# A two-layer decoder trunk on one core: seven products in every step of the middle MLP passes, with part of the weights' low parts made by adding DMAs

## The chip, the cores and the metric

The kernel runs on one core of a Trainium2 chip. The metric is the device time of one execution in microseconds, as the median of several runs. The profiled execution has a span, from its first to its last instruction, which is a few microseconds shorter than the time of a run.

The engines are called by the profile's short names: PE is the matrix engine TensorE and PEld its weight loads, DVE is VectorE, ACT is ScalarE, POOL is GpSimd and SP is SyncE, which issues most of the DMAs. PSUM is the memory that PE writes to, eight banks of 512 columns of float32; SBUF is the working memory; both have 128 partitions.

## What is computed

The input is 256 positions of width 2048, in float32. There are two layers: a gated short convolution and an MLP, then latent attention and an MLP. After each of the four sub-layers stands x <- LN(alpha * x + f(x)). What matters here is the MLP, of which there are two:

```
def sq_relu_mlp(x, w1, w2):
    return jnp.square(jax.nn.relu(x @ w1)) @ w2        # w1: 2048 x 8192, w2: 8192 x 2048

h = layer_norm(ALPHA * h + mix, ln_g[layer, 0], ln_b[layer, 0])
h = layer_norm(ALPHA * h + sq_relu_mlp(h, mlp_w1[layer], mlp_w2[layer]), ln_g[layer, 1], ln_b[layer, 1])
```

## The kernel before

**Precision by parts.** PE multiplies in the type float32r, which holds fewer bits than float32. Each operand is therefore split into a high part (the value rounded to float32r) and a low part (the value minus the high part), and a product is three matmuls: high by high, high by low, low by high. `split` (L125) makes the two parts: ACT casts the high part (L127), DVE subtracts (L128). For the weights this is done on the chip, for every half of 128 x 1024 numbers that is loaded.

**The stream of weights.** `stream` is the list of all weight pieces in the order of their use. `take` (L183) hands out the next one and, before that, emits the loading and splitting of the pieces that are up to LOOK = 5 steps ahead. A raw half lands in a ring of RAW = 5 buffers (`raws`), its two parts in a ring of WA = 8 pairs (`whl`). The loads are issued on SP's queue (L138), which is in order: a load waits there until its buffer is free.

**An MLP.** `mlp` (L575) runs over NQ = 8 slices q of the hidden dimension, 1024 columns each. A pass has two halves. In the first, `products` multiplies the input by w1 in eight chunks of 128 hidden columns; `hidden` (L713) reads each chunk from PSUM (`whole`, L355 and L356), applies relu and square (L718, L719) and splits the result. In the second half the hidden values are multiplied by the slice of w2 and added to the sums of the output, 256 x 2048.

**Passes with seven products.** In the passes q = 1 to 6 (FAST) a 2 x 2 block product uses seven block products instead of eight, in the manner of Strassen and Winograd. `form` (L703) builds the four sums and differences of the hidden values (S1 to S4). `prepare` (L141) builds those of the weights: a step of seven loads two raw halves, the blocks 11 and 22 in the one, 21 and 12 in the other; DVE forms T1 and T3 (L162), T2 (L166) and T4 (L169), and three pairs of 1024 columns and one of 512 are split. `fast_products` (L343) issues the seven products, each by `dot` (L297), three matmuls of 512 columns (L300, L302, L303). They go into seven sums named "1" to "7", one PSUM bank each. Four of these (OWN: "1", "5", "7", "6") are kept apart over the passes in a buffer `sums`, the others are kept in blocks of the accumulator `acc`; `fold` (L669) adds the four to the accumulator in the last pass.

**The two groups.** The 2048 output columns are worked on as two groups g of 1024. In every middle pass group 1 comes first, with four steps in the order MIXED = "sssp": three steps of seven ("s") and one plain step ("p") that multiplies the same operands with eight products, without the sums and differences; one of its matmuls is split in two. Then come four steps of seven for group 0. The partial sums change place at each switch: `resumed` (L608) copies a sum from SBUF into its PSUM bank (L612), `put_back` (L615) copies it back (L616), both on ACT, and `keep` (L618) adds it to SBUF on DVE (L624).

**The residual.** `xres` holds the residual stream, 128 x 16 x 256 float32, in SBUF throughout. In the first MLP `begin` (`prepare_chunks`, L798) scales and centres its chunks for the next layer norm during the last pass, and `to_wide` (L776) adds the MLP's output to them. In the second MLP `turn_residual` (L1024) brings it to the accumulator: PE transposes it (L1027) into PSUM, DVE adds it to `acc` (L1028). That is spread over the passes 1 to 4, eight transposes in each, after the first chunk.

**Order.** The order of the instructions on each engine is set by a scheduler that places them by their dependences; an engine then works through its own queue in order and waits where an operand or a buffer is not there yet.

## Time and profile before

| | |
|---|---|
| Runs (three) | 1997.85, 1999.94, 2000.18 us; median 1999.94 us |
| Span of the profiled execution | 1994.9 us |
| Mean granted clock of PE | 1.000 |
| Loads of raw halves of w2 for the steps of seven | 168 of 512 KB, median 3.9 us from issue to landing |
| Loads of the other MLP weights | 344 of 512 KB, median 4.5 us |
| Bytes moved by DMA | 385.85 MB |

A page of the profile gives the busy time of each engine, the chain of work that ended last, the groups of instructions and the DMA issues. Matmuls are pipelined, so the busy time of a single one (0.39 us for 512 columns) is longer than the distance from its start to the next one's start; distances are what counts. The same holds on a smaller scale for DVE and ACT. In the rows, a name such as `lo<-raw,hi` is the written tile and the tiles read, and L128 is line 128 of the kernel.

### The profile page before, as it was taken

What the parts mean: (1) busy time and instruction counts of PE and PEld (TensorE: products, weight loads), DVE (VectorE), ACT (ScalarE), POOL (GpSimd) and SP (SyncE); (2) the same over time, 40 slices, a digit from 0 to 9 for tenths busy, and PEclk for the clock granted to TensorE, in tenths of its full rate; (3) what the DMA queues carried; (4) which work ended last, traced back from release to release, by engine and by line L of the source; (5) the groups of instructions that cost most, each with busy time, mean ns of one, the idle gap of its engine ahead of it and who ended that gap; (6) DMA issues with size and microseconds to landing.
All of it is one profiled execution on the core that took longest, in us unless ns stands there. A gap on an engine that the chain in (4) does not pass through costs nothing.

```text
span 1994.9 us, 30180 instructions
## 1 busy us (share of the span) xinstructions
PE 1987.7 (100%) x11110; PEld 1737.2 (87%) x11110; DVE 1709.4 (86%) x2555; ACT 1354.9 (68%) x2154; POOL 2.3 (0%) x21
## 2 busy tenths in 40 slices
PE   9999999999999999999999999999999999999998
PEld 8888888988888888888889998898888888888886
DVE  8667667797999989989978988777899999999985
ACT  6444445586778778777756755558677787887772
POOL 0000000000000000000000000000000000000000
PEclk9999999999999999999999999999999999999999
DMA  8666666565657466574855543656464656656483
GB/s 318 205 191 187 190 190 190 179 193 157 212 170 251 148 216 221 177 243 147 281 171 159 170 140 123 201 180 195 146 233 155 232 161 220 222 178 233 150 269 130
DMA packets 106853, 385.85 MB, mean 193 GB/s; under 512 B 11857, under 2 KB 12625, under 8 KB 106449
## 3 DMA queue, kind: packets, MB, share of 16 engines
q1 hardware_dynamic: 106560, 383.79, 59.5%
q8 instruction: 87, 1.43, 0.3%
q14 instruction: 62, 0.50, 0.1%
q10 hardware_dynamic: 144, 0.13, 0.0%
HBM read 381.78 MB, written 2.10 MB: 192 GB/s over the span
## 4 chain that ended last, share of the span: by engine, by line
PE 98%; DVE 1%; ACT 1%; issue 0%; DVEq 0%; ACTq 0%
PE ps_u L215 20%; PE ps_l L215 13%; PE ps_u L219 10%; PE ps_l L219 7%; PE ps_f L300 4%; PE ps_f L303 4%; PE ps_f L302 4%; PE ps_r L303 4%; PE ps_r L302 4%; PE ps_r L300 4%; PE ps_d L300 2%; PE ps_d L302 2%; PE ps_d L303 2%; PE ps_w L249 2%; PE ps_w L248 2%; PE ps_w L247 2%
## 5 line engine op out<-in xcount | busy, mean ns | idle before, releaser
L128 DVE TENSOR_TENSOR lo<-raw,hi 128x1024 fp32r<-128x1024 f32 x710 | 861.8, 1220 | 190.6 <-ACT hi L127 119.9
L127 ACT CAST hi<-raw 128x1024 fp32r<-128x1024 f32 x710 | 741.8, 1051 | 247.4 <-PE ps_l L215 98.1
L215 PE MATMUL ps_u<-xhl,hi 128*128 128x512 f32 x1792 | 621.7, 392 | 0.0
L219 PE MATMUL ps_u<-xhl,lo 128*128 128x256 f32 x1792 | 498.2, 279 | 0.0
L215 PEld LDWEIGHTS ps_u<-xhl,hi 128*128 128x128 f32 x1792 | 334.5, 187 | 73.6 <-ACT acc L595 0.2
L219 PEld LDWEIGHTS ps_u<-xhl,lo 128*128 128x128 f32 x1792 | 338.1, 189 | 1.8
L215 PE MATMUL ps_l<-xhl_a,hi 128*128 128x512 f32 x704 | 244.1, 393 | 0.0
L219 PE MATMUL ps_l<-xhl_a,lo 128*128 128x256 f32 x704 | 195.4, 279 | 0.0
L215 PEld LDWEIGHTS ps_l<-xhl_a,hi 128*128 128x128 f32 x704 | 132.1, 188 | 29.9
L219 PEld LDWEIGHTS ps_l<-xhl_a,lo 128*128 128x128 f32 x704 | 131.9, 188 | 0.2
L127 ACT CAST hi_t<-raw_t 128x1024 fp32r<-128x1024 f32 x84 | 88.5, 1054 | 45.8 <-DVE raw_t L162 41.4
L162 DVE TENSOR_TENSOR raw_t<-raw,raw 128x1024 f32<-128x1024 f32 x84 | 102.3, 1218 | 1.8 <-DMA raw<-in_w2f_dram 1.5
L128 DVE TENSOR_TENSOR lo_t<-raw_t,hi_t 128x1024 fp32r<-128x1024 f32 x84 | 102.4, 1219 | 0.2
L718 ACT ACTIVATE fp<-fp 128x256 f32<-128x256 f32 x96 | 40.0, 416 | 63.2 <-DVE fp L356 62.6
L215 PE MATMUL ps_l<-z,hi 128*128 128x512 f32 x240 | 82.4, 391 | 0.0
L300 PE MATMUL ps_d<-hi,h 128*128 128x512 f32 x192 | 75.0, 391 | 0.0
L302 PE MATMUL ps_d<-lo,h 128*128 128x512 f32 x192 | 75.0, 390 | 0.0
L303 PE MATMUL ps_d<-hi,h 128*128 128x512 f32 x192 | 74.8, 389 | 0.0
L249 PE MATMUL ps_w<-xd,hi 128*128 128x258 f32 x256 | 72.7, 284 | 0.0
L248 PE MATMUL ps_w<-xd,lo 128*128 128x258 f32 x256 | 72.3, 282 | 0.0
L247 PE MATMUL ps_w<-xd,hi 128*128 128x258 f32 x256 | 72.3, 282 | 0.0
L215 PE MATMUL ps_l<-oT,hi 128*128 128x512 f32 x208 | 71.3, 391 | 0.0
(296 smaller groups left out, 3963.7 us busy)
## 6 DMA issues: line engine op xcount, KB each, us to landing
raw<-in_w_dram SPq DMA_DIRECT2D x344, 512.0 KB, 4.5
raw<-in_w2f_dram SPq DMA_DIRECT2D x168, 512.0 KB, 3.9
raw<-in_w_in_dram SPq DMA_DIRECT2D x88, 512.0 KB, 4.2
raw<-in_w_out_dram SPq DMA_DIRECT2D x32, 512.0 KB, 3.7
raw<-in_w_o_dram SPq DMA_DIRECT2D x32, 512.0 KB, 4.2
raw<-in_w_kv_dram SPq DMA_DIRECT2D x10, 512.0 KB, 3.7
raw<-in_w_q_dram SPq DMA_DIRECT2D x8, 512.0 KB, 4.0
raw<-in_w_uk_dram SPq DMA_DIRECT2D x8, 512.0 KB, 3.9
```

Source lines behind the costliest of these rows:

```text
L127: nc.scalar.copy(hi, src)
L128: nc.vector.tensor_tensor(lo, src, hi.bitcast(F32), ALU.subtract)
L162: nc.vector.tensor_tensor(t.rearrange(two, a=2), b12.unsqueeze(1).to_broadcast([P, 2, BW]), r1.rearrange(two, a=2), ALU.subtract)
L215: nc.tensor.matmul(ps, w[blk // 8][0][:, blk % 8, :], x, start=first, stop=False)
L219: nc.tensor.matmul(ps[:, :T], w[blk // 8][1][:, blk % 8, :], x[:, :T], start=False, stop=last)
L247: nc.tensor.matmul(ps[:, :W], hi, x[k][:, :W], start=k == 0, stop=False)
L248: nc.tensor.matmul(ps[:, :W], lo, x[k][:, :W], start=False, stop=False)
L249: nc.tensor.matmul(ps[:, :W], hi, x[k][:, W:], start=False, stop=k == NC - 1)
L300: nc.tensor.matmul(ps, x[0], w[0], start=first, stop=False, skip_group_check=onto)
L302: nc.tensor.matmul(ps[:, at], x[0], w[1][:, at], start=False, stop=False, skip_group_check=onto)
L303: nc.tensor.matmul(ps, x[1], w[0], start=False, stop=last, skip_group_check=onto)
L718: nc.scalar.activation(f, f, AF.Relu)
```

## The change

All middle passes now use seven products in all eight steps; the plain step and its code are gone. The two groups alternate: a pass begins with the group with which the pass before it ended, and the sums "3", "1", "5" and "7" of that group stay in PSUM over the boundary. The sums "3" and "1" always start fresh and are added to SBUF by DVE (`keep`, now for all ways back), the others are copied in and out by ACT. In the last of the first group's four steps the sums are exchanged one by one, behind each product (`turn`).

In four of the eight steps of a middle pass (ADDED: the last two of the first group, the first two of the second) the low part of the first raw half is made in another way: ACT casts the high part, ACT writes its negative to the low part, and a DMA on POOL's queue adds the weights from DRAM to it. `form` writes its sums and differences into one tile beside the hidden values, and one split of 896 columns makes all seven left factors; relu and square work on two chunks at a time.

The rings are deeper: seven raw buffers instead of five, nine pairs instead of eight. The place for it comes from `sums`, which now takes the place of `xres`. In the first MLP the residual is scaled and centred in pass 1 already, stored to DRAM (`parked`), and loaded back in the last pass. In the second MLP all its transposes are in the first four chunks of pass 1.

```diff
-RAW, WA = 5, 8
+RAW, WA = 7, 9
-MIXED = "sssp"
-EVEN = (QC - 1, "22")
+ADDED = ((0, 2), (0, 3), (1, 0), (1, 1))
+FRESH = ("3","1")
...
+    def groups(q):
+        return (1, 0) if (q - FAST[0]) % 2 == 0 else (0, 1)
...
-            for j, kind in enumerate(MIXED):
-                out += [(w2f[l, q, 1, j, 0], w2f[l, q, 1, j, 1])] if kind == "s" else \
-                    halves(w2[l, q, 2, j]) + halves(w2[l, q, 3, j])
-            out += [(w2f[l, q, 0, j, 0], w2f[l, q, 0, j, 1]) for j in range(QC // 2)]
+            for i, g in enumerate(groups(q)):
+                for j in range(QC // 2):
+                    out.append((w2f[l, q, g, j, 0], w2f[l, q, g, j, 1]) + (("added",) if (i, j) in ADDED else ()))
...
-        def finished(r, name):
+        def finished(r, name, src=None):
             hi, lo = parts(name)
-            split(hi, lo, tiled(r))
+            if src is None:
+                split(hi, lo, tiled(r))
+            else:
+                nc.scalar.copy(hi, tiled(r))
+                nc.scalar.activation(lo, hi.bitcast(F32), AF.Copy, scale=-1.0)
+                nc.gpsimd.dma_start(lo, tiled(src), accum_op=ALU.add)
             out.append((hi, lo))
...
-        sums = fast.tile([P, 4, 2, BW], F32, name=f"sums{idx}")
+        sums = None
...
+        def begun_sum(p, g, name, bank):
             ps = psum(name, bank)
-            if q != FAST[0] or p not in OWN:
+            if not new_sum(p):
                 nc.scalar.copy(ps, place(p, g))
             return ps
...
+        def keep(p, g, ps, since):
             at = place(p, g)
-            if q == FAST[0] and p in OWN:
+            if p not in FRESH or (since == FAST[0] and p in OWN):
                 nc.scalar.copy(at, ps)
             else:
                 nc.vector.tensor_tensor(at, at, ps, ALU.add)
...
+            def turn(p):
+                keep(p, first, ps[p], max(q - 1, FAST[0]) if p in order[:4] else q)
+                i = order.index(p) + 1
+                if i < len(order):
+                    begin_next(order[i], banks[p])
...
+            for j in range(n):
+                if j == n - 1:
+                    begin_next(order[0], spare)
+                fast_products(ps, h, j, new - held_on if j == 0 else (), ps if j == n - 1 else (),
+                              set(ps) - (new - held_on), turn if j == n - 1 else None)
+            for j in range(n):
+                fast_products(after, h, j, new if j == 0 else (), after if j == n - 1 else (),
+                              set(order) - new, end if j == n - 1 else None)
...
+            def form(j, u):
+                a21, a11, a12, s1, s2, s4 = (u[:, i * P:(i + 1) * P] for i in (0, 1, 3, 4, 6, 7))
+                two = u.rearrange("p (i c) -> p i c", c=P)
+                nc.vector.tensor_tensor(s1, a21, u[:, 2 * P:3 * P], ALU.add)
+                nc.vector.tensor_tensor(two[:, 5:7, :], two[:, 0:5:4, :], a11.unsqueeze(1).to_broadcast([P, 2, P]),
+                                        ALU.subtract)
+                nc.vector.tensor_tensor(s4, a12, s2, ALU.subtract)
+                f = factors[j // 2][:, j % 2]
+                split(f[:, 0, :], f[:, 1, :], u[:, P:])
...
-                    if extra and m == 0 and q <= NB:
+                    if extra and q == FAST[0] and m < NB:
                         for t in range(2):
-                            extra(block, q - 1, t, busy[2 + t])
+                            extra(block, m, t, busy[2 + t])
+                    if begin and q == FAST[0]:
+                        begin(range(max(2 * m, 1), 2 * m + 2))
+                        nc.sync.dma_start(parked[:, 2 * m:2 * m + 2, :], held_x[0][:, 2 * m:2 * m + 2, :])
+                    if q == FAST[0] and m == QC - 1:
+                        sums = act.tile([P, 4, 2, BW], F32, tag="xres", name=f"sums{idx}")
...
+                if begin and q == NQ - 1:
+                    held_x[0] = act.tile([P, NC, T], F32, tag="xres", name="xback")
+                    for k in range(0, NC, 4):
+                        nc.sync.dma_start(held_x[0][:, k:k + 4, :], parked[:, k:k + 4, :])
```

More of the change, by code (lines that the diff above doesn't have):

```diff
@@ L440, in wide @@
         def wide(self, m):
-            d, x, g = xres[:, m, :], self.xd[m], self.gain(m)[0]
+            d, x, g = held_x[0][:, m, :], self.xd[m], self.gain(m)[0]
             nc.scalar.activation(x[:, :T], d, AF.Copy, scale=g)
@@ new lines, in down_pairs, with begin_next, end @@
+        def down_pairs(h, ps, banks, spare):
+            first, second = groups(q)
+            n = QC // 2
+            order = [p for p, _, _ in FACTORS]
+            stay = order[:4] if q < FAST[-1] else []
+            new = {p for p in order if new_sum(p)}
+            after, place_of = {}, {}
+            def begin_next(p, bank):
+                after[p], place_of[p] = begun_sum(p, second, f"ps_f{p}", bank), bank
+            def turn(p):
[3 more added lines that the diff above has]
+                    begin_next(order[i], banks[p])
+            def end(p):
+                if p not in stay:
+                    keep(p, second, after[p], q)
+            held_on = set(order[:4]) if q > FAST[0] else set()
+            for j in range(n):
+                if j == n - 1:
[5 more added lines that the diff above has]
+                              set(order) - new, end if j == n - 1 else None)
+            if stay:
+                return [banks[order[-1]]] + [place_of[p] for p in order[4:]], {p: after[p] for p in stay}, \
+                    {p: place_of[p] for p in stay}
+            return [banks[order[-1]]] + [place_of[p] for p in order[:3]], {}, {p: place_of[p] for p in order[3:]}
@@ L773, in mlp @@
             else:
-                busy, free = down_pairs(h, forms, busy, free, begun)
+                busy, sums_in, places = down_pairs(factors, sums_in, places, busy[3])
     def to_wide(block, put, h):
```

146 lines of the change are left out of this document (53 added, 93 removed).

## The prediction

> **What bounds the kernel now.** I read the page first: the busy times and the chain that ended last.
>
> ```profile
> span 1994.9 us, 30180 instructions
> PE 1987.7 (100%) x11110; PEld 1737.2 (87%) x11110; DVE 1709.4 (86%) x2555; ACT 1354.9 (68%) x2154; POOL 2.3 (0%) x21
> PE 98%; DVE 1%; ACT 1%; issue 0%; DVEq 0%; ACTq 0%
> ```
>
> TensorE (PE) is 98% of the chain, so a change pays only if PE issues less or waits less. The profiled execution's span is 1994.9 us and the median of the runs is 1999.94 us; I carry this difference of 5.0 us unchanged.
>
> Next, the twelve middle passes (q = 1 to 6 of each MLP), cut at the same matmul of successive passes. The columns are length, busy time of PE, PEld, DVE, ACT and POOL with counts, granted clock, DMA share, GB/s.
>
> ```profile
> core 0: us, PE busy (x) PEld busy (x) DVE busy (x) ACT busy (x) POOL busy (x), PEclk, DMA share, GB/s
> 453.75:536.98 83.23, 83.23 (x430) 71.28 (x429) 73.42 (x97) 58.98 (x91) 0.00 (x0) 1.00 0.52 162
> 620.21:703.43 83.22, 83.22 (x429) 71.27 (x429) 80.15 (x104) 66.50 (x102) 0.00 (x0) 1.00 0.63 206
> 869.88:954.04 84.16, 83.70 (x430) 71.13 (x429) 79.04 (x103) 66.35 (x103) 0.00 (x0) 1.00 0.59 199
> 1647.81:1731.90 84.09, 84.09 (x438) 71.88 (x437) 79.86 (x104) 66.61 (x102) 0.00 (x0) 1.00 0.62 201
> 620.20:664.60 44.40, 44.40 (x257) 39.04 (x256) 41.69 (x59) 35.52 (x57) 0.00 (x0) 1.00 0.70 236
> 664.60:703.40 38.80, 38.80 (x175) 32.20 (x174) 38.45 (x46) 30.99 (x46) 0.00 (x0) 1.00 0.55 173
> ```
>
> A pass takes 83.22 us at full clock with no gap. VectorE (DVE) is busy for 80.15 of it, and in the second half (the last row, the products with w2; the row above it is the first half, eight chunks with w1) for 38.45 of 38.80: it is nearly a second bound. The passes of the last MLP with eight transposes of the residual take 84.09. One pass took 84.16, and the waits of PE's weight loads in the first MLP say why:
>
> ```profile
> PEld ps_f L300 <- ACT acc L616: 0.9, 1, 0.9
> PEld ps_f L300 <- ACT ps_f L612: 0.3, 1, 0.3
> ```
>
> A copy of a partial sum between PSUM and SBUF, queued on ScalarE (ACT), came late. 84.16 - 83.22 = 0.94 us lost.
>
> **The change, part by part. PE.** PE's timeline of the second half shows both kinds of step: start, duration, what.
>
> ```profile
> 511.49 0.39 PE L300 MATMUL ps_r<-hi,h 128*128 128x512 f32 x1
> 515.12 0.40 PE L302 MATMUL ps_r<-lo,h 128*128 128x256 f32 x2
> 516.74 0.39 PE L303 MATMUL ps_r<-hi,h 128*128 128x512 f32 x1
> 516.96 0.39 PE L300 MATMUL ps_f<-hi,forms 128*128 128x512 f32 x1
> 521.72 0.39 PE L300 MATMUL ps_f<-hi,forms 128*128 128x512 f32 x1
> ```
>
> The plain step ("p", eight products of three matmuls, one of them split in two) lasts from 511.49 to 516.96: 5.47 us. A step of seven products lasts from 516.96 to 521.72: 4.76 us, or 0.227 a matmul and 0.68 a product. The change makes every step one of seven: 5.47 - 4.76 = 0.71 us a pass, 12 x 0.71 = 8.5 us. This is the first term. Nothing covers it or takes it back, as long as PE stays without gaps; the rest asks whether it does.
>
> **DVE.** Prices are from start to start, back to back, for 256, 128, 1024 and 512 columns:
>
> ```profile
> 654.28 0.42 DVE L356 TENSOR_TENSOR fp<-ps_u,t 128x256 f32<-128x256 f32 x1
> 654.61 1.22 DVE L128 TENSOR_TENSOR lo<-raw,hi 128x1024 fp32r<-128x1024 f32 x1
> 658.74 0.28 DVE L710 TENSOR_TENSOR sf<-fp,sf 128x128 f32<-128x128 f32 x1
> 658.95 0.68 DVE L128 TENSOR_TENSOR t<-raw,t 128x512 fp32r<-128x512 f32 x1
> 682.47 1.22 DVE L128 TENSOR_TENSOR lo_t<-raw_t,hi_t 128x1024 fp32r<-128x1024 f32 x1
> 683.61 0.68 DVE L169 TENSOR_TENSOR raw<-raw 128x512 f32<-128x512 f32 x1
> 684.21 1.22 DVE L162 TENSOR_TENSOR raw_t<-raw,raw 128x1024 f32<-128x1024 f32 x1
> ```
>
> These are 0.33, 0.21, 1.14 and 0.60 us. A pass issues now 46 instructions of 1024 columns, 32 of 512, 8 of 256 and 16 of 128: 52.4 + 19.2 + 2.6 + 3.4 = 77.6, near the 80.15 of the window. Afterwards there are 44 of 1024 (one step of seven more brings 4 but the plain step's 2 go, and the adding DMAs take 4), 26 of 512, 4 of 896 (about 1.0 by the line between 512 and 1024), 12 of 256 and 8 of 128: 50.2 + 15.6 + 4.0 + 4.0 + 1.7 = 75.5, or 2.1 less in a pass that is 0.7 shorter. DVE keeps its place just under PE.
>
> **ACT.** Again start to start:
>
> ```profile
> 695.64 1.05 ACT L127 CAST hi<-raw 128x1024 fp32r<-128x1024 f32 x1
> 696.59 0.61 ACT L127 CAST t<-raw 128x512 fp32r<-128x512 f32 x1
> 697.11 1.05 ACT L127 CAST hi<-raw 128x1024 fp32r<-128x1024 f32 x1
> ```
>
> and a copy between PSUM and SBUF, by its group in the pass from 620, has the busy time of a 512-column cast:
>
> ```profile
> L612 ACT COPY ps_r<-sums 128x512 f32<-128x512 f32 x4 | 2.3, 579 | 0.0
> ```
>
> A 1024-column instruction costs 0.95, a 512 one 0.52. ACT gains one cast and four sign flips (lo = -hi) of 1024: +4.8. The sums that stay in PSUM over the pass boundary, or start fresh, save eight copies: 8 x 0.52 = -4.2. Wider relu, square and cast instructions save about 1.5 by the line through the two prices. ACT stays near 66 of 82.5 us: no term.
>
> **The adding DMAs.** Per pass four of 512 KB, on POOL's queue, which is otherwise empty. The trace has no DMA that adds and none from POOL, so the length L from issue to landing must be bounded. The nearest rows are the DMA issues, with KB and median us to landing, then the first queue's packets, and the DMA share of the window 620 to 704 in 40 slices:
>
> ```profile
> out_dram<-acc SPq DMA_DIRECT2D x8, 256.0 KB, 2.4
> raw<-in_w2f_dram SPq DMA_DIRECT2D x168, 512.0 KB, 3.9
> first<-in_w_first_dram SPq DMA_DIRECT2D x2, 1024.0 KB, 11.2
> q1 hardware_dynamic: 106560, 383.79, 59.5%
> DMA  8999999799287207530591287850490077285798
> ```
>
> From below L is 3.9, a plain load of this size. From above I take 11.2, the slowest issue shown, of twice the bytes. I take 7.8, two loads' worth, since an add has to read both operands.
>
> What L may be follows from the order in which the changed kernel queues its work. Count from PE's start of the first of the eight steps. The tightest is the fifth: PE needs its low part at 4 x 4.76 + 0.23 = 19.3. On ACT its sign flip stands behind the cast of the third step's fourth factor, which waits for one of two buffers until PE ends the first step, at 4.76; then come that cast (0.52), three casts of 1024 and the flip (3.8): 9.1. Lead: 10.2 us. The others have 11 to 12. With L = 7.8 no PE time is lost, with 11.2 it is 1.0 a pass.
>
> [...]
>
> Bandwidth: 383.79 MB are 732 halves of 512 KB; 0.595 x 1994.9 / 732 = 1.62 us of all 16 engines each. Four adds cost 6.5 (as a load) to 13.0 (double). They fall in the second half, where the share is 0.55 of 38.8 us and 17.5 us are idle; the full slices at the window's start are another stretch. No term.
>
> **The residual.** In the first MLP eight stores of 256 KB (2.4 us each by the row of the output) and four loads of 512 KB stand in SP's queue among the weight loads. A store waits for the chunk's DVE step, and the loads behind it are for work two chunks of w1 later (2 x 44.4 / 8 = 11 us), which covers 3.9 us. The four loads back stand behind eight halves of w2 and are used two output blocks later. Fifteen centring steps move from the last pass to q = 1, where DVE has the room (73.42 busy in that pass). No term.
>
> In the last MLP the 32 transposes move from four passes into the first four chunks of one:
>
> ```profile
> 1400.24 0.93 PE L1027 MATMUL turned<-id_t,xres 128*128 128x128 f32 x7
> 1400.77 1.29 DVE L1028 SCALAR_TENSOR_TENSOR acc<-turned,acc 128x512 f32<-128x512 f32 x2 [0.91 <-PE turned L1027]
> 1401.27 0.37 ACT L355 COPY t<-ps_u 128x256 f32<-128x256 f32 x1
> ```
>
> PE's own cost is the same. But the PSUM banks are those of the chunks in work, so five times PE must wait for DVE's reading: none where the interposed matmuls cover it, at most 1.29 (both readings) each: 0 to 6.5 us. DVE is idle for about half of that stretch, so I take 1.0.
>
> **Sum.** -8.5 (matmuls) - 0.9 (the late copy) + 1.0 (transposes) = -8.4. Span 1994.9 - 8.4 = 1986.5; median 1999.94 - 8.4 = 1991.5.
>
> **Rivals.** First: the switch between the two halves of the columns becomes a wait. Ten PSUM copies of 0.52 on ACT and two adds of 0.60 on DVE must pass while PE does seven products (4.76 us), each for the product that follows one step later. ACT needs 5.2 us there, so it runs slightly late, with a step's slack. For it speaks the late copy above; against it that before has 24 such copies a pass and lost 0.94 once in twelve. With 0.5 us a pass, 12 x 0.5 = 6.0: 1997.5, within the noise.
>
> Second: the transposes at their upper end, 1991.5 + 5.5 = 1997.0. For it: the banks are the same ones. Against: DVE's idle time there.
>
> Third, slower: the adds land after their lead. The place is the low part of the fifth step; it decides from L = 10.2, and eats the gain at 10.2 + 8.4 / 12 = 10.9. If the operands' reads and the write run one after the other, L = 3 x 3.9 = 11.7 and PE waits 1.5 a pass: 12 x 1.5 = 18, 2009.5. For it: no add is in the trace, and the second half has the least slack of DVE, which would be behind too. Against: ten us is more than twice a load.
>
> Fourth, the change doesn't do what it says: POOL's work for the adds holds up DVE, whose 4 x 1.14 us saved come back. DVE then has 80.1 of 82.5 us, and a delay of 1 us a pass gives 2003.5. POOL's row shows 2.3 us in all, so nothing speaks for or against.
>
> **How the numbers follow.** Forecast 0.62; first and second together 0.15, a third of which is still faster by enough; third 0.18; fourth 0.05. A difference of 0.2% (4.0 us) is about what this kernel's runs can tell. Faster: 0.62 + 0.05 = 0.67. Same: 0.10. Slower: 0.23. The forecast's own range is 1988 (no transposes' cost, and the 1997.85 of the fastest run) to 1996. The range for 8 in 10 goes to 2005: it takes in the first two rivals, the fourth, and the third up to L = 11.3.
>
> **What will show it.** Windows of a middle pass should read 82.5 us, with DVE near 78 and ACT near 66. The stretch of seven-product steps should be 8 x 4.76 = 38.1. PE should wait for no low part of an adding DMA; the issue-to-landing time of these DMAs should be 4 to 10 us. The first pass of the last MLP should be near 82.5 + 3.5 + 1.0. The forecast is wrong if a pass is longer than 83 us, if PE's waits name an adding DMA or a PSUM copy in most passes, or if DVE's 1024-column instructions grow while POOL works.

## The result, and the profile after

The kernel before took 2000.06 us (median of four runs), the changed kernel 2033.68 us (2030.75 to 2038.88, four runs): 1.0168 times as long, with a 95% interval of 1.0150 to 1.0186. The forecast was 1991.5, its range for 8 in 10 went to 2005: the kernel became slower where faster was forecast. The profiled execution's span is 2028.9 us.

From the page of the changed kernel: span, busy times, queues, the chain that ended last, and issues with the median us to landing.

```profile
span 2028.9 us, 30032 instructions
PE 1990.3 (98%) x11062; PEld 1731.3 (85%) x11062; DVE 1684.2 (83%) x2461; ACT 1355.3 (67%) x1998; POOL 44.6 (2%) x69
q0 software_dynamic: 6912, 25.17, 7.3%
PE 74%; DVE 11%; DMA 8%; issue 4%; ACT 2%; DVEq 0%; SPq 0%; POOLq 0%; POOL 0%; ACTq 0%
lo<-in_w2f_dram POOLq DMA_DIRECT2D x48, 512.0 KB, 5.9
```

DVE has 25 us less to do, ACT as much as before: both as counted. But PE is only 74% of the chain where it was 98%; DVE and DMAs have entered it. The 48 adds cost 0.073 x 2028.9 / 48 = 3.1 us of all 16 engines each, against 1.62 for a plain load.

What PE's weight loads, and in the last row DVE, waited for (us in total, times, longest):

```profile
PEld ps_f L318 <- DMA lo<-in_w2f_dram: 37.9, 19, 3.7
PEld ps_f L316 <- ACT ps_f L641: 1.4, 2, 0.9
PEld ps_f L316 <- DVE acc L650: 1.3, 1, 1.3
PEld ps_u L231 <- DVE acc L1050: 0.6, 2, 0.5
DVE raw_t L182 <- DMA raw<-in_w2f_dram: 43.0, 28, 2.9
```

The adding DMAs are nearly all of PE's waits. For DVE raw halves came late, 43.0 us in all, against 1.5 us before. The windows show where PE lost its time: the second half of a middle pass (the steps of seven), the whole pass, and the second half of a later one. The columns are those of the prediction's windows.

```profile
672.25:712.16 39.91, 38.76 (x171) 31.36 (x169) 36.88 (x44) 33.17 (x44) 2.64 (x3) 1.00 0.82 224
627.86:712.16 84.30, 83.15 (x426) 70.48 (x424) 77.34 (x94) 66.15 (x89) 3.51 (x4) 1.00 0.73 220
840.00:882.95 42.95, 38.73 (x171) 31.38 (x170) 36.63 (x44) 33.27 (x45) 2.63 (x3) 1.00 0.80 224
```

The first half is as before (84.30 - 39.91 = 44.39). The second was forecast at 38.1 and takes 39.91 here and 42.95 in the later pass. POOL's queue in that half, from the second add on, with start, duration and what ended the idle time:

```profile
844.18 0.86 POOL L164 DMA_DIRECT2D lo<-in_w2f_dram  x1 [5.25 <-ACT lo L163]
853.19 0.89 POOL L164 DMA_DIRECT2D lo<-in_w2f_dram  x1 [8.14 <-ACT lo L163]
861.42 0.88 POOL L164 DMA_DIRECT2D lo<-in_w2f_dram  x1 [7.35 <-ACT ps_f L641]
```

ACT's and PE's timelines of the same stretch; L163 is the sign flip of the third and of the fourth add:

```profile
850.35 0.94 ACT L133 CAST h_5a<-fp 128x896 fp32r<-128x896 f32 x1 [1.26 <-DVE fp L721]
...
851.72 1.06 ACT L163 ACTIVATE lo<-hi 128x1024 fp32r<-128x1024 f32 x1
...
854.70 1.06 ACT L163 ACTIVATE lo<-hi 128x1024 fp32r<-128x1024 f32 x1
```

```profile
859.08 0.39 PE L316 MATMUL ps_f<-hi,h_5c 128*128 128x512 f32 x1
861.16 0.50 PE L318 MATMUL ps_f<-lo,h_5c 128*128 128x512 f32 x1 [1.69 <-DMA lo<-in_w2f_dram]
...
868.76 0.50 PE L318 MATMUL ps_f<-lo,h_5c 128*128 128x512 f32 x1 [2.53 <-DMA lo<-in_w2f_dram]
```

PE begins the fifth step at 859.08 and then waits 1.69 us for the third add, issued at 853.19. The fourth add's flip has ended at 855.76, but the add is issued only at 861.42, when the third has landed; so PE waits again, 2.53 us, in the sixth step. (The profile names a copy of ACT as what ended POOL's idle time there; the run with more descriptor memory, below, shows that it was the third add.) Over all twelve passes, by the same rows, PE waited at the fifth step eight times, 14.1 us in all, and at the sixth eleven times, 15.7 us (waits of the matmuls; those of the weight loads, which run ahead, sum to the 37.9 above).

### The profile page after: what moved, and what is told of

Same layout as the page of the kernel before. It is cut to its first block, busy times and chain, and to the rows that moved or that the text cites. A ratio compares the mean times of both kernels' runs of the same rounds, so it can differ in the third digit from the quotient of the medians.

```text
span 2028.9 us, 30032 instructions
## 1 busy us (share of the span) xinstructions
PE 1990.3 (98%) x11062; PEld 1731.3 (85%) x11062; DVE 1684.2 (83%) x2461; ACT 1355.3 (67%) x1998; POOL 44.6 (2%) x69
## 3 DMA queue, kind: packets, MB, share of 16 engines
q0 software_dynamic: 6912, 25.17, 7.3%
## 4 chain that ended last, share of the span: by engine, by line
PE 74%; DVE 11%; DMA 8%; issue 4%; ACT 2%; DVEq 0%; SPq 0%; POOLq 0%; POOL 0%; ACTq 0%
PE ps_u L231 15%; PE ps_l L231 13%; PE ps_u L235 7%; PE ps_l L235 7%; DMA lo<-in_w2f_dram 4%; PE ps_f L318 3%; DMA raw<-in_w2f_dram 3%; PE ps_f L319 3%; PE ps_f L316 3%; DVE lo L134 2%; PE ps_d L316 2%; PE ps_d L318 2%; PE ps_d L319 2%; DVE raw_t L182 2%; PE ps_w L265 2%
## 5 line engine op out<-in xcount | busy, mean ns | idle before, releaser
L134 DVE TENSOR_TENSOR lo<-raw,hi 128x1024 fp32r<-128x1024 f32 x662 | 799.5, 1220 | 191.6 <-ACT hi L133 121.2
L133 ACT CAST hi<-raw 128x1024 fp32r<-128x1024 f32 x662 | 684.8, 1052 | 253.2 <-PE ps_l L231 103.6
L182 DVE TENSOR_TENSOR raw_t<-raw,raw 128x1024 f32<-128x1024 f32 x96 | 117.0, 1219 | 43.5 <-DMA raw<-in_w2f_dram 43.0
L133 ACT CAST hi_t<-raw_t 128x1024 fp32r<-128x1024 f32 x96 | 100.6, 1048 | 41.6 <-DVE raw_t L182 32.0
L134 DVE TENSOR_TENSOR lo_t<-raw_t,hi_t 128x1024 fp32r<-128x1024 f32 x96 | 116.9, 1217 | 1.4 <-ACT hi_t L133 1.4
L164 POOL DMA_DIRECT2D lo<-in_w2f_dram x48 | 42.3, 881 | 1610.3 <-DVE fp L721 550.6
L133 ACT CAST t<-raw 128x512 fp32r<-128x512 f32 x96 | 59.3, 618 | 23.7 <-DVE raw L189 23.7
L733 ACT ACTIVATE fp<-fp 128x512 f32<-128x512 f32 x96 | 60.2, 627 | 19.3 <-DVE fp L374 19.0
L265 PE MATMUL ps_w<-xd,hi 128*128 128x258 f32 x256 | 72.7, 284 | 0.0
```

The source lines that it names most:

```text
L133: nc.scalar.copy(hi, src)
L134: nc.vector.tensor_tensor(lo, src, hi.bitcast(F32), ALU.subtract)
L164: nc.gpsimd.dma_start(lo, tiled(src), accum_op=ALU.add)
L182: nc.vector.tensor_tensor(t.rearrange(two, a=2), b12.unsqueeze(1).to_broadcast([P, 2, BW]), r1.rearrange(two, a=2), ALU.subtract)
L265: nc.tensor.matmul(ps[:, :W], hi, x[k][:, W:], start=False, stop=k == NC - 1)
L733: nc.scalar.activation(u[:, :2 * T], u[:, :2 * T], function)
```

## The experiments

Times are medians, each beside the kernel before in the same series (1997.8 to 2001.2 us). All edits are to the changed kernel; those with 1024 bytes of descriptor memory take its place from the buffers of the hidden chunks outside the middle passes, as in the second diff. "Descriptor memory" is what the kernel sets with `dynamic_dma_scratch_size`; the change has 512 bytes, as before.

### No adds, more descriptor memory, other places, flips alone

```diff
-ADDED = ((0, 2), (0, 3), (1, 0), (1, 1))
+ADDED = ()
```

> All low parts are again made by VectorE's subtraction; everything else of the change stays. Theory 1 (the adding DMAs run one at a time, the third and fourth of a pass land after PE needs them; this is the whole loss): the 37.9 us that the weight loads waited for adding DMAs go, 2033.7 - 37.9 = 1996, or 1996 to 2000 if VectorE, with 4 x 1.14 us more a pass, is late now and then. Theory 2 (the raw loads come late because of the deeper use of the rings and the alternating groups, and with them the casts and the sign flips): VectorE still waits about 40 us for raw halves, its work is larger, and the time stays above 2010. Theory 3 (the residual's transposes, its stores and the copies at the switch cost most): above 2010 with PE's waits at those places.

2017.9 us, 1.0079 times before (1.0064 to 1.0094). The waits for adds are gone, but theory 1 missed the time. Theories 2 and 3 had it (above 2010) and not the rows: DVE waited 6.8 us for raw halves, not 40, and PE's weight loads waited 6.7 us for ACT's casts, 6.6 for DVE's subtractions and 5.7 for the adds of the switch. Its window of a middle pass:

```profile
623.61:708.28 84.67, 84.40 (x425) 70.23 (x424) 81.41 (x99) 62.69 (x85) 0.00 (x0) 1.00 0.62 200
```

DVE is busy for 81.41 of 84.67 us, where a pass without waits takes 82.5. Without adds, seven products in every step leave DVE so little room that PE waits for it and for what stands behind it: DVE has to be relieved of something.

```diff
-    nc = _bacc.Bacc("TRN2", target_bir_lowering=False, num_devices=1, dynamic_dma_scratch_size=512)
+    nc = _bacc.Bacc("TRN2", target_bir_lowering=False, num_devices=1, dynamic_dma_scratch_size=1024)
...
-                f = tmp.tile([P, T], F32, tag="fh", name="fh", bufs=3)
+                f = tmp.tile([P, T], F32, tag="fh", name="fh", bufs=2)
```

> The memory in which POOL writes the descriptors of its DMAs is 1024 bytes a partition instead of 512 (made free by two instead of three buffers for the hidden chunks of the other passes). Theory 1, in the form that this memory holds the descriptors of one add only: two adds can be in flight, POOL issues the next less than 5.9 us after the one before where its sign flip is done, the 19 waits of PE fall to 6 or fewer and the time to about 2005. Theory 1 in the form that POOL or the DMA engines themselves take one add at a time, whatever the memory: the gap between issues stays at 5.9 us or more and the time within 3 us of 2033.7. Theory 2 (late raw loads and late flips): the issues follow the flips, the time stays above 2025.

2013.9 us: 20 less than the change. Its third and fourth add in the pass shown above, and PE's waits:

```profile
848.07 0.89 POOL L164 DMA_DIRECT2D lo<-in_w2f_dram  x1 [8.01 <-ACT lo L163]
851.05 0.88 POOL L164 DMA_DIRECT2D lo<-in_w2f_dram  x1 [2.09 <-PE ps_f L319]
```

```profile
PEld ps_f L318 <- DMA lo<-in_w2f_dram: 17.4, 10, 3.3
```

The fourth add is now issued 2.98 us after the third, while that is in flight; in the change no two are closer than 5.9 us. What vanished are the waits at the sixth step (11 become 1); the eight at the fifth stay (10 waits of the weight loads are left, where theory 1 allowed 6). So one add at a time was the limit of that memory, and half of the loss.

```diff
-ADDED = ((0, 2), (0, 3), (1, 0), (1, 1))
+ADDED = ((0, 1), (0, 3), (1, 1), (1, 3))
```

> The same four adds a pass, but in every second step instead of four in a row. Theory 1 (one add at a time): the sign flips come 9.5 us apart, more than the 5.9 us of an add, so none queues behind another; each still has 5.9 to 8.7 us against a lead of about 6 to 10, so PE's waits fall to under 10 us in all and the time to about 2003. Theory 2 (late raw loads and late flips): the waits for adds move to the new places, at least 25 us of the 37.9 stay, and the time is above 2018. If the transfers that the adds make, and not their order, are the cost, the time stays near 2033.

2076.4 us, the waits for adds 61.7 us, 21 times. Theory 1 missed; theory 2 had the direction (waits at the new places, above 2018), not the size, and the raw halves were not the reason: DVE waited only 14.8 us for them. No add queued here, and the two of the first group met no wait, but the sixth and the eighth step waited up to 4.8 us. The eighth step's flip stands on ACT behind the switch's ten PSUM copies and ends 29.8 us after the start of the steps, 3.7 before PE needs the low part; what the copies cost is settled below. The sixth step's stands ahead of the copies and ends at 17.5, a lead of 6.5, where the adds there took 7.7 us in the median.

```diff
-                nc.gpsimd.dma_start(lo, tiled(src), accum_op=ALU.add)
```

> ScalarE's cast and sign flip stay, the adding DMA behind them is left out, so the low part of these four halves a pass holds only the negative of the high part (the weights are not added). Theory 1: PE waits for no flip, VectorE has its 4.9 us a pass less work and the time is what the change would give if the adds were free: 1991 to 1996. Theory 2 (late flips): the wait is handed to ScalarE's flip and at least half of the 37.9 us stays: above 2010. If it comes out as fast as the kernel with no adds at all, the relief of VectorE is worth nothing.

1993.2 us, 0.9959 times before (0.9945 to 0.9973): the change with adds that cost nothing. A whole middle pass, its second half, and the first pass of the second MLP, where the residual's transposes are:

```profile
621.30:703.82 82.52, 82.52 (x426) 70.66 (x425) 78.25 (x95) 66.67 (x89) 0.00 (x0) 1.00 0.63 208
665.69:703.82 38.13, 38.13 (x171) 31.54 (x170) 36.69 (x44) 33.20 (x44) 0.00 (x0) 1.00 0.59 180
1393.94:1481.40 87.46, 86.98 (x457) 73.98 (x456) 75.05 (x96) 60.67 (x81) 0.00 (x0) 1.00 0.47 145
```

These are the forecast's numbers (82.5, DVE 78, ACT 66, 38.1, and 87.0). The loss of the change against this run, 2033.7 - 1993.2 = 40.5 us by the medians and 2028.9 - 1992.0 = 36.9 by the profiled spans, is that of the adding DMAs, which are the only difference: by PE's timelines the twelve second halves take 498.6 us in the change and 461.2 here. ACT's and PE's timelines of a later pass also show the lead that the fifth step's add has when nothing disturbs it (the left-out rows are three casts of 1024 columns):

```profile
836.35 0.61 ACT L133 CAST t<-raw 128x512 fp32r<-128x512 f32 x1
...
839.95 0.95 ACT L133 CAST h_5a<-fp 128x896 fp32r<-128x896 f32 x1
840.79 0.61 ACT L133 CAST t<-raw 128x512 fp32r<-128x512 f32 x1
841.31 1.06 ACT L163 ACTIVATE lo<-hi 128x1024 fp32r<-128x1024 f32 x1
```

```profile
830.72 0.39 PE L315 MATMUL ps_f<-hi,h_5c 128*128 128x512 f32 x1
...
850.03 0.39 PE L317 MATMUL ps_f<-lo,h_5c 128*128 128x512 f32 x1
```

This second half starts at 830.72 (first row). The flip ends at 842.37, 11.65 us later (forecast: 9.1), and PE needs the low part at 850.03: a lead of 7.66 us, not 10.2 (the need is 19.3 after the start, as forecast). Over the twelve passes of this run the flip ends 10.1 to 12.2 us after the start, and 15.7 in the first pass.

### The same DMAs without the add, and fewer adds

```diff
-                nc.gpsimd.dma_start(lo, tiled(src), accum_op=ALU.add)
+                nc.gpsimd.dma_start(lo, tiled(src))
```

> The same four DMAs from POOL's queue in the same places, behind the same casts and flips, but they copy the weights over the low part instead of adding (the low part of these halves then holds the whole weights). If the add's second read makes it long and fills the descriptor memory: a copy lands in 3.9 to 4.5 us as SP's loads do, the share of the 16 engines falls from 7.3% to about 4%, a second copy is issued while the first is in flight, PE waits under 5 us in all and the time is 1993 to 1998. If POOL's queue itself is slow and takes one DMA at a time: 5.4 us or more to landing, gaps of 5.9 us or more between issues, and a time above 2020.

1992.7 us, 0.9967 times before (0.9956 to 0.9978), with one wait of 0.3 us for these DMAs. Its queue and issue rows:

```profile
q0 software_dynamic: 6912, 25.17, 4.1%
lo<-in_w2f_dram POOLq DMA_DIRECT2D x48, 512.0 KB, 4.6
```

With the same bytes written from the same queue, a copy takes 4.6 us (3.7 to 5.8) and an add 5.9 (5.4 to 8.7); in engine time 1.7 against 3.1 us. The copies are issued as close as 2.98 us with 512 bytes of descriptor memory:

```profile
842.01 0.53 POOL L164 DMA_DIRECT2D lo<-in_w2f_dram  x1 [8.14 <-ACT lo L163]
844.99 0.53 POOL L164 DMA_DIRECT2D lo<-in_w2f_dram  x1 [2.45 <-ACT lo L163]
```

It is the add that is long and alone, not POOL's queue. At the fifth step the flips end as late as in the change (a lead of 4.9 to 9.2 us, counted to the need at 19.3), and the copies fit since they land in 4.2 to 5.3 us, where the change's adds took 5.8 to 8.2 there, 7.4 in the median. An add has 1.8 times a copy's engine time (3.1 / 1.7) and 1.3 times its time to landing (5.9 / 4.6).

```diff
-ADDED = ((0, 2), (0, 3), (1, 0), (1, 1))
+ADDED = ((0, 2), (1, 0))
```

> Only two adds a pass: for the third and the fifth step; the other low parts by VectorE. In the kernel with the flips alone, the flip for the fifth step ended 7.66 us before PE needs that low part (not 10.2 as predicted), and nothing is in flight before this add. Theory A (the fifth step's add loses because its lead is short and it runs into the other adds and the loads): alone it takes 5.4 to 6 us, PE's waits for adds fall to under 4 us in all, VectorE has 2 x 1.14 us more a pass than with four; between the flips alone (1993) and no adds (2018), about 2000. Theory B (an add here takes 7 to 9 us whatever else is in flight): PE still waits 1 to 2 us at the fifth step in most passes, 10 to 20 us in all, and the time is above 2010.

2000.6 us, 1.0005 times before (0.9996 to 1.0015), and no wait for an add: theory A's outcome, but not for its reason. The page's time to landing, and the fifth step's flip in the pass whose second half starts at 830.99:

```profile
DMA to landing us min/median/max: 5.5/5.9/9.5
838.46 1.06 ACT L163 ACTIVATE lo<-hi 128x1024 fp32r<-128x1024 f32 x1
```

At the fifth step alone the adds took 7.6 us in the median and up to 9.5, no less than in the change, though nothing else of POOL was in flight. What changed is the lead: with the fourth step's flip gone, the fifth's ended 8.5 to 10.4 us after the start (8.53 in the row shown, ahead of the cast of the hidden values). PE needs the low part at 19.3, so the lead is 8.9 to 10.8. With the lead that the prediction counted, the adds fit.

```diff
-ADDED = ((0, 2), (0, 3), (1, 0), (1, 1))
+ADDED = ((0, 2), (0, 3), (1, 1))
```

> Three adds a pass: third, fourth and sixth step; the fifth step's low part is made by VectorE. The flip for the sixth step ended 9.4 us before the need in the kernel with the flips alone. Theory A (short lead of the fifth step's add, and the add of the sixth queued behind it): no wait for an add is left (under 3 us in all), VectorE has 1.14 us a pass more than with four, time 1994 to 2001. Theory B (an add takes 7 to 9 us always): still under 9.4, so no waits either. Theory C (the traffic of the adds makes the raw loads and with them VectorE late): VectorE's wait for raw halves stays above 35 us and the time above 2008.

> Three adds as in the run that leaves out the fifth step's, with the descriptor memory of 1024 bytes. Where only the sixth step's add is left behind a gap of two steps, the memory should not matter: the same time as with 512 bytes within 3 us, if theory A holds. If the add of the fourth step still queues behind that of the third at 512 bytes and costs PE or ACT time there, this one is faster by more than 3 us.

2011.2 us, and 2012.9 with 1024 bytes of memory: the memory does not matter once the adds are apart, as expected. But both waited for the sixth step's add, eight times, 13 us in all, against the expectation. With the fifth step's subtraction back on DVE, the sixth's flip is in most passes 6.5 us ahead of its use and no longer 9.4: a lead read from one kernel did not carry over to another.

```diff
-ADDED = ((0, 2), (0, 3), (1, 0), (1, 1))
+ADDED = ((0, 0), (0, 2), (1, 0))
```

> Three adds a pass with a step between them: first, third and fifth step; descriptor memory as in the change. Theory A (an add costs PE time only where it queues behind another or its lead is under about 7 us): none queues, the fifth step's has 7.7 us as in the run with two adds, PE waits under 3 us for adds in all. VectorE has one subtraction a pass more than with four: between 1993 (flips alone) and 2000.6 (two adds), about 1997. Rival: the traffic of the adds (the first falls among the loads for w1) makes loads late, the time is 2003 or more and PE waits for adds or VectorE's waits for raw halves exceed 30 us.

```diff
-ADDED = ((0, 2), (0, 3), (1, 0), (1, 1))
+ADDED = ((0, 0), (0, 1), (0, 2), (0, 3))
```

> Four adds a pass in the four steps of the first group, where the pairs of buffers come free while PE still works on the chunks of w1; descriptor memory of 512 bytes. Theory A: the steps follow each other as before, so flips that come less than 6 us apart queue; the last of the four is then late: PE waits 5 to 25 us for adds, 2000 to 2015. If the leads there are long enough to cover one add's queue (10 us or more), no waits, and 1993 to 1998. If the adds' traffic alone were the loss (rival), above 2020.

> The same places with the descriptor memory of 1024 bytes: two adds can be in flight. Theory A: at most as many waits as with 512 bytes, and the time 1993 to 1999. Rival (traffic): no better than with 512 bytes, above 2010.

2011.6, 2015.7 and 2014.2 us. No wait for an add in any, and yet slow. The first two fit neither theory; the third has its rival's numbers (no better than with 512 bytes, above 2010). The waits of the three adds apart:

```profile
PEld ps_f L318 <- DVE lo_t L134: 9.2, 11, 1.0
PEld ps_f L316 <- ACT ps_f L641: 8.2, 13, 0.9
PEld ps_f L316 <- DVE acc L650: 6.0, 7, 1.8
```

PE waits now for DVE and for the copies of the switch. DVE has less to do in all than with two adds (1698.8 against 1709.4 us busy), but with these places its subtractions stand together in the last steps. That this is the reason fits the rows; it was not tried by itself. The adds' traffic is the rival that is left: DVE waited 25.8 us for raw halves here and 45.2 and 42.6 us in the two runs with four adds, against 10.9 with two adds, though also 25.1 in the run with copies, which lost nothing.

```diff
-RAW, WA = 7, 9
+RAW, WA = 5, 10
```

> The change with ten pairs of buffers instead of nine and five raw halves instead of seven (the same memory). Theory A1 (the flip of the fifth step waits for the low buffer that PE reads in the second step, so the ring of pairs sets the lead): the flip comes up to 1.6 us earlier, PE's waits for adds fall from 37.9 to 15 to 25 us, the time to about 2015. Theory A2 (the flip stands behind other work on ScalarE and VectorE, whose raw halves come late): with five raw halves VectorE waits longer than 43 us for them, the waits of PE grow, and the time is 2035 or more.

2051.5 us, the time of A2: with five raw halves DVE waited 62.7 us for loads, and PE for DVE and ACT. The waits of the weight loads for adds fell to 1.7 us, as A1 would have it; but as PE was late everywhere, the adds had more time too, so the run does not show whether the ring of pairs sets the lead.

### Half the bytes

Here the add makes only the block 11 (256 KB), DVE the block 22.

```diff
-                nc.scalar.activation(lo, hi.bitcast(F32), AF.Copy, scale=-1.0)
-                nc.gpsimd.dma_start(lo, tiled(src), accum_op=ALU.add)
+                nc.scalar.activation(lo[:, :4], hi[:, :4].bitcast(F32), AF.Copy, scale=-1.0)
+                nc.gpsimd.dma_start(lo[:, :4], tiled(src)[:, :4], accum_op=ALU.add)
+                nc.vector.tensor_tensor(lo[:, 4:], tiled(r)[:, 4:], hi[:, 4:].bitcast(F32), ALU.subtract)
```

> The change's four adds, each for the block 11 alone (256 KB, 512 columns); the low part of the block 22 is made by VectorE (0.60 us each). Theory A (length against lead): an add of half the bytes lands in 3 to 4.5 us, under the 7.7 us lead of the fifth step even behind the one before it, and the next is issued sooner; PE's waits for adds fall from 37.9 us to under 5. VectorE's relief is half of four whole adds, as with two adds; time 1995 to 2003. Theory B (the cost of an add is per DMA and not by bytes): 5.4 us or more to landing, waits of 15 us or more, above 2015.

1996.7 us, 0.9993 times before (0.9983 to 1.0002), theory A: no wait for an add, in the very places and with the memory of the change. Both sides moved: at the fifth step the adds took 5.6 us in the median, and the flips ended 9.2 to 10.1 us after the start, so the lead was longer too.

```profile
lo<-in_w2f_dram POOLq DMA_DIRECT2D x48, 256.0 KB, 4.4
```

Next the half add moves to block 21, needed with the fifth product, in four steps and in all eight:

```diff
+        def begun_21(r, name, src):
+            hi, lo = parts(name)
+            nc.scalar.copy(hi[:, :4], tiled(r)[:, :4])
+            nc.scalar.activation(lo[:, :4], hi[:, :4].bitcast(F32), AF.Copy, scale=-1.0)
+            nc.gpsimd.dma_start(lo[:, :4], tiled(src)[:, :4], accum_op=ALU.add)
+            out.append((hi, lo))
...
         finished(t, f"{i}_t")
+        if len(stream[i]) == 3:
+            begun_21(r2, f"{i}_2", stream[i][1])
```

> In the same four steps the add makes the low part of the block 21 (256 KB), which PE needs with the fifth product of a step, 4 x 0.68 = 2.7 us later than the first pair; its cast and flip come before VectorE's differences. Theory A: no wait for an add (under 1 us), VectorE relieved by 4 x 0.54 us a pass, time 1995 to 2003. Rival (ScalarE: one instruction more in a step, and the flip before other casts, makes the casts late): PE waits for casts or for PSUM copies, above 2005.

> The same in all eight steps of a pass: as many bytes added as in the change, in eight DMAs of 256 KB spread evenly, and VectorE relieved evenly by 8 x 0.54 = 4.3 us a pass. Theory A: adds land 4 us after their issue and 4.8 us apart, with about 9 us of lead, so no waits for adds; time 1992 to 1997, faster than the kernel before and the change. Rival 1 (ScalarE): about 8 x 0.6 us more work a pass, waits for casts and PSUM copies, 2000 or more. Rival 2 (traffic): the adds in every step make the raw halves late, above 2010.

2011.1 and 2089.9 us, both missed: 17.2 and 71.3 us of waits for adds. The adds took 5.3 and 5.6 us, and with all eight they were issued 5 to 10 us apart where a step takes 4.76. With all eight, PE waits in every pass once at the seventh step and once at the eighth; for the run with four the reason was not followed up.

> The run with a 256 KB add for the block 21 in all eight steps, with 1024 instead of 512 bytes of descriptor memory. If one add at a time was the cause of its 71 us of waits: issues come closer than the time to landing, PE's waits for adds fall to under 25 us and the time from 2090 to 2000 to 2025. If the flips come late whatever the memory (rival): the issues stay 5 to 10 us apart, time above 2070.

2067.5 us, 54.2 us of waits: between the two, nearer the rival. The memory took 22 us off, as in the second run; issues are still 3.5 to 10 us apart.

```diff
-ADDED = ((0, 2), (0, 3), (1, 0), (1, 1))
+ADDED = tuple((i, j) for i in range(2) for j in range(4))
```

with 1024 bytes and the block 11 again:

> 256 KB adds for the block 11 in all eight steps, with 1024 bytes of descriptor memory: VectorE relieved by 4.3 us a pass, evenly. Theory A (one at a time and the lead are all that an add has to meet): two can be in flight, 4.4 us each, lead 7 us or more: PE waits under 5 us for adds, time 1992 to 1997, faster than the kernel before. Rival (the leads of the last steps, from the sixth on, are shorter still, as the run with adds in every second step showed at the last step): 10 us or more of waits, 2003 or more.

2052.9 us; the rival. PE waits once in each pass, 48.1 us in all, at the seventh step. POOL's queue and ACT's timeline of one pass show why:

```profile
778.73 0.86 POOL L164 DMA_DIRECT2D lo<-in_w2f_dram  x1 [4.34 <-ACT lo L163]
792.08 0.89 POOL L164 DMA_DIRECT2D lo<-in_w2f_dram  x1 [12.49 <-DVE raw L190]
```

```profile
782.66 1.07 ACT L649 COPY sums<-ps_f 128x512 f32<-128x512 f32 x2
...
787.13 0.63 ACT L642 COPY ps_f<-acc 128x512 f32<-128x512 f32 x1
...
791.02 0.66 ACT L163 ACTIVATE lo<-hi 128x512 fp32r<-128x512 f32 x1
```

From 782.66 to 787.65 ACT does the ten copies of the switch, and the seventh step's casts and flip stand behind them: 13 us between two adds.

```diff
-ADDED = tuple((i, j) for i in range(2) for j in range(4))
+ADDED = ((0, 0), (0, 1), (0, 2), (0, 3), (1, 0), (1, 1))
```

> 256 KB adds for the block 11 in the first six steps of a pass, whose flips are queued on ScalarE ahead of the copies of the switch; 1024 bytes of descriptor memory. If those copies made the seventh step's add late: no waits for adds (under 3 us in all, against 48 with eight), and 1993 to 1998 by VectorE's relief of 6 x 0.54 us a pass. If the number of adds or their traffic was the reason: 15 us or more of waits remain and the time is above 2010. If the relief is spread unevenly (the subtractions that are left stand in the last two steps, as in the run with the first four steps): no waits for adds, but waits for VectorE and PSUM copies, 2003 to 2015.

1994.9 us (1993.4 to 1997.3, eleven runs), 0.9980 times before (0.9971 to 0.9989): faster than both kernels, and without any wait for an add. Its adds land after 3.8 us in the median. The window of a middle pass:

```profile
618.34:701.19 82.85, 82.82 (x425) 70.58 (x424) 78.66 (x100) 66.22 (x92) 5.21 (x6) 1.00 0.70 224
```

Six adds of half the bytes, all ahead of the switch's copies on ACT. Two were allowed in flight, but only two of the 72 adds were issued while another was on its way, so the larger memory did little here. The last two steps keep their whole subtractions on DVE, and the loss that the third expectation feared from that did not come.

## Why the prediction was wrong

- **Matmuls, -8.5; late copy, -0.9; transposes, +1.0.** Right. With the flips alone the pass takes 82.52, the second half 38.13, the pass with the transposes 87.46 (82.52 + 4 x 0.87 for the transposes themselves + 1.46).
- **The sum and the 5.0 us carried.** With the flips alone the median is 8.1 us under the kernel before of its series (forecast 8.4), but the span only 1994.9 - 1992.0 = 2.9 under the span before. Its first pass of the first MLP takes 85.35 instead of 82.5, with weight loads waiting 3.0 us for DVE's sums, and stretches outside the middle passes are some 2 us longer: the moved residual and the deeper rings may not have been free, as "no term" had it. Whether the centring steps moved into that pass are the reason was not tried. That the medians differ by more than the spans comes from the kernel before: its runs lie between 1996.0 and 2002.8, and the span of the profiled one is near the lower end. In the later profiles the run's time is 1.7 to 2.1 us over its span, not 5.0.
- **DVE and ACT.** Their busy times were right. That DVE is "a second bound" was right and its consequence not drawn: 48 more subtractions, 4 a pass, cost 2017.9 - 1993.2 = 24.7 us, and three adds placed in other steps (2011.6) were slower than two (2000.6).
- **L of an add, 7.8 taken, 3.9 to 11.2 bounds.** Two loads' worth was an estimate from the plain load's 3.9. It is above the median of 5.9 over all places, but right for the place that decides: at the fifth step the change's adds took 7.4 in the median. L was not what failed.
- **"Lead: 10.2 us."** This step failed. The flip of the fifth step's low part was counted 9.1 us after the start of the steps. In the pass shown it is 11.65 with adds that cost nothing: the cast it counts from starts 0.87 us later, and a cast of the hidden values (0.85), a second 512-column cast (0.52) and small gaps, which the count left out, stand before the flip. In the same pass of the change it ended 12.78 after the start, since DVE had waited 2.07 us for a raw half. The lead is 7.7 to 6.5 us, and the third add took 8.0 there (853.19 to 861.16): PE waits. Over the twelve passes PE waits in exactly those eight in which the lead was 4.2 to 6.8 us, and not in the four with 7.0 to 9.2.
- **"The others have 11 to 12."** The second failure, as large. The sixth step's flips ended 5.9 to 9.1 us before the need, most of them early enough for the 5.6 to 8.7 that its adds took; but the adds were issued 2 to 6 us after the flips. Each add was given its own lead from its own flip, as if all could be in flight together. They run one at a time, so the fourth add starts when the third lands. With twice the descriptor memory this half of the loss (20 us) is gone.
- **Third rival, 2009.5 with L = 11.7.** Place and direction were right (the fifth step's low part), the price not: it was to decide from L = 10.2, and decided with a lead of 4.2 to 6.8, in eight passes of twelve, with the queue's share beside it in eleven.
- **First rival (copies at the switch).** In the change 1.4 us, and 1.3 for the switch's adds. In other placings it decides: 8.2 us of waits with three adds apart, and the seventh step's 13 us gap.
- **Second rival (transposes).** 0.6 us of waits for DVE's reading, the lower end. **Fourth (POOL holds up DVE).** DVE's 1024-column subtraction stays at 1.22 us, with and without adds; no.
- **Bandwidth, no term.** With copies in place of adds, 1992.7 us: no cost to see. With the adds the second half's DMA share is 0.80 to 0.82 instead of 0.59, and DVE waits 43.0 us for raw halves instead of 25.1 with copies and 20.1 with flips alone. That shortened the lead: in the pass shown the fifth step's flip ended 11.65 us after the start with flips alone, 12.41 with copies and 12.78 with adds.

Open: why 512 bytes of descriptor memory hold up a second add and not a second copy. The queue's row has the same 6912 packets and 25.17 MB for 48 adds and for 48 copies, and no run here shows what the memory holds.

## What to carry to other kernels

A DMA that takes over an engine's work puts a latency where the engine had none (5.9 us in the median here); its lead has to be counted through the whole in-order queue of the engine that releases it, with everything that stands there (11.65 us to the flip here, not 9.1), and the DMAs of one queue have to be checked for running one at a time (the change's adds were issued at least 5.9 us apart, the copies in their place as close as 2.98). Where several engines are within a few per cent of the bound, the total of saved work did not tell the time here (three adds apart against two); that the steps in which it is saved decide was argued, not shown. When a lead is a microsecond or two short, halving the transfer can be worth more than leaving it out: in the same places four adds of 256 KB took 1996.7 us, four of 512 KB 2033.7 and none 2017.9; six of 256 KB gained 0.2% on the kernel before.

## What was not expected of the hardware

A wait of PE can cost more than its length: here one of 3.23 us cost 1.5 us more. PE's timeline of the changed kernel around its longest wait, and the windows behind it:

```profile
520.12 0.79 PE L318 MATMUL ps_f<-lo,h_1c 128*128 128x512 f32 x1 [3.23 <-DMA lo<-in_w2f_dram]
520.71 0.63 PE L319 MATMUL ps_f<-hi,h_1c 128*128 128x512 f32 x1
521.13 0.63 PE L316 MATMUL ps_f<-hi,h_1c 128*128 128x512 f32 x1
...
523.22 0.39 PE L319 MATMUL ps_f<-hi_t,h_1c 128*128 128x512 f32 x1
```

```profile
520.12:522.10 1.98, 1.98 (x5) 1.59 (x6) 1.31 (x3) 1.98 (x5) 0.89 (x1) 0.50 1.00 410
```

After 3.23 us of waiting the granted clock is 0.50 and matmuls start 0.42 us apart instead of 0.227. From 520.12 to 523.22 seven of them take 3.1 us instead of 1.6: another 1.5 us lost. With adds in every second step, where waits reached 4.8 us, the mean clock of the whole run fell to 0.986.

The length of the wait alone does not decide. After this kernel's three waits of 2.5 us the matmuls go on at their old distance, but 1.1 us after the end of one of 2.04 us the clock halves too:

```profile
1566.51 0.50 PE L318 MATMUL ps_f<-lo,h_2c 128*128 128x512 f32 x1 [2.04 <-DMA lo<-in_w2f_dram]
1568.32 0.63 PE L318 MATMUL ps_f<-lo_t,h_2c 128*128 128x512 f32 x1
```

By the clock records the two slow stretches start at 519.73 and 1567.62, last 3.413 us each and are 307 x 3.413 us apart. In every run whose passes have such stretches, their starts lie on a grid of this step. Windows cut on that grid (length, PE's busy time, clock, DMA share, GB/s), the one before the second slow stretch and the one with the larger part of one of the 2.5 us waits:

```profile
1564.21:1567.62 3.41, 1.37 (x7) 1.00 1.01 353
611.89:615.30 3.41, 1.65 (x7) 1.00 0.61 179
```

The wait of 2.04 us lies whole in one grid window and leaves PE idle for 2.04 of 3.41 us; the longer one is cut by the border of two windows, and the larger part leaves 1.76. Over the ten runs that have such stretches in their passes, cut on their grids from 450 to 1960 us of the span, all 51 windows at full clock with 1.89 us or more of idle PE were followed by half clock, and of those with less only two (1.72 and 1.79). So a little over half of such a window idle, 1.89 of 3.413 us, was enough here.
